# Moving one head's gate projection behind the last retention projection, and three tables behind the first weight loads

## The chip, the cores and the metric

The program runs on one core of one Trainium2 chip, in one launch. The metric is the device time of the program in microseconds (us); several executions are timed and the median is taken. TensorE multiplies matrices, VectorE and ScalarE work on whole tiles of 128 partitions, GpSimd takes a share of the elementwise work, and SyncE issues nearly all transfers between HBM and SBUF. Each engine runs its own instructions strictly in the order in which they stand in its program, and waits on semaphores for the others.

## What is computed

Two layers of a hybrid encoder over 512 tokens of width 1024. Each layer has four retention heads and four stick-breaking attention heads of width 128 that share one input projection and one output projection, then a SwiGLU feed-forward part; norms stand ahead of each part, and one more at the end.

```python
for l in range(DEPTH):                       # 2
    h = rms_norm(x, norm1_g[l])
    rq, rk, rv, rg, sq, sk, sv = jnp.split(h @ w_in[l], IN_SPLITS, axis=-1)   # 512 columns each
    ret = chunk_retention(apply_rotary(heads(rq)), apply_rotary(heads(rk)), heads(rv))
    ret = from_heads(head_group_norm(ret, ret_norm_g[l])) * jax.nn.silu(rg)
    sb  = stick_breaking(heads(sq), heads(sk), heads(sv))
    sb  = from_heads(head_rms_norm(sb, sb_norm_g[l]))
    x = x + jnp.concatenate([ret, sb], axis=-1) @ w_out[l]
    h = rms_norm(x, norm2_g[l])
    x = x + (jax.nn.silu(h @ w_gate[l]) * (h @ w_up[l])) @ w_down[l]
return rms_norm(x, final_g)
```

The gate `rg` has one block of 128 columns for each retention head. A head's gate is wanted only when that head's retention output is there, since `silu(rg)` multiplies it.

## The kernel before

Everything is float32. To reach that precision each operand is split into a high part (`hi`, a cast on ScalarE) and a low part (`lo`, a subtraction, on VectorE or GpSimd), and each product of two operands is three matmuls: hi·hi, lo·hi, hi·lo. The normed input stands in `hhi`, `hlo` (eight tiles of 128x512). The weights come in units of 512 KB, each of 128x1024, in the order of their use (`block_plan`). A unit is loaded into `wraw` (three buffers), cast to `whi` by ScalarE (L124) and subtracted to `wlo` by VectorE (L125). A cast must wait until TensorE has done with the unit that lay three units earlier in the same buffer.

In a layer's attention the order of TensorE's work is written out by hand. The main stream is: values of the stick-breaking heads (SV); for each stick head its query, key, and one retention gate (SQ, SK, RG); values of the retention heads (RV); for each retention head its query and key (RQ, RK); then the output projection, first the half of the stick heads, then that of the retention heads. One projection of a head is 24 matmuls of 512 columns and one unit of weights. Side tasks are put into this stream by the class `Stream`: a task is queued with a delay (`pe.later`) and written into TensorE's order when the stream has advanced so far. Heads are counted from 0 to 3.

The side tasks of retention head h are:

- `retain`: block `z` = scores of keys and queries, ten groups in three PSUM banks. The first matmul reads the high parts `qhi`, `khi`; the third is the first to read `klo`. VectorE then multiplies by the decay table `dec` (L552), and the product is split into `pthi`, `ptlo`.
- `mixed` (L557): `o` = values times weights, then VectorE's `m` = `o` times gain times gate (L561), and `normed`: ScalarE squares `o` (L460), casts the square to `shi`, GpSimd takes `slo`.
- `finish`: two matmuls of `ones_r` with `shi` and `slo` sum the squares into `o`; then `rsqrt`: on ScalarE a logarithm (L298) and an exponential (L299), both written as `r`, on VectorE `u`, `u`, `rn`; then `m` is scaled and split into `mhi`, `mlo` for the output projection.

Ahead of `retain`, `rotated` evacuates each query or key projection with three VectorE operations (L414 to L416, tiles `t`), GpSimd adds them, ScalarE casts (`qhi`, `khi`), GpSimd subtracts (`qlo`, `klo`).

ScalarE's functions come from table sets. A SiLU needs one set, logarithm and exponential another; `table_set` puts an explicit load into the program, and where a function stands under a set that doesn't hold it, another load is put in front of it. All four gates are passed through SiLU by one instruction of 2048 columns between two loads (L217, L220).

The order of TensorE is fixed by hand; that of VectorE, ScalarE, GpSimd and SyncE is set by a scheduler when the program is built. The two decay tables that fit (`dec`, two buffers) are loaded head by head in each layer (L537); the rotary tables `cosrs`, `sinrs` at the start of each layer's attention (L340, L341).

Of the kernel before, what the change touches and what calls it, by code (L numbers as in the profile page):

```python
# [10 lines left out]
F32 = mybir.dt.float32  # L11
# [3 lines left out]
ALU = mybir.AluOpType  # L15
# [9 lines left out]
NH = 4  # L25
# [11 lines left out]
# the triangle of score blocks, by bank: block rows of [query, key], and of [key, query]  # L37
# [7 lines left out]
def block_plan():  # L45
    """Weight blocks in the order of their use: (tensor, layer, k tile, column, width)."""
    plan = []

    def cols(name, l, col):
        return [(name, l, k, col, P) for k in range(KT)]  # L50

    for l in range(L):
        plan += [("w_in", l, k, SV, 512) for k in range(KT)]
        for h in range(NH):
            for c in (SQ, SK, RG):
                plan += cols("w_in", l, c + h * HD)
        plan += [("w_in", l, k, RV, 512) for k in range(KT)]
        for h in range(NH):
            plan += cols("w_in", l, RQ + h * HD) + cols("w_in", l, RK + h * HD)
        for d in range(KT):  # L60
            plan += [("w_out", l, NH + k, d * P, P) for k in range(NH)]
        for d0 in range(0, KT, 4):
            ds = range(d0, d0 + 4)
            plan += [("w_out", l, k, d * P, P) for d in ds for k in range(NH - 1)]
            plan += [("w_out", l, NH - 1, d * P, P) for d in ds]
        for k in range(KT):
            for f in range(2):
                plan += [("w_gate", l, k, f * P, P), ("w_up", l, k, f * P, P)]
        for half in range(2):
            fs = range(half * FH, half * FH + FH)  # L70
            for f in fs:
                if f >= 2:
                    plan += cols("w_gate", l, f * P) + cols("w_up", l, f * P)
            if l < L - 1:
                for d in range(KT):
                    plan += [("w_down", l, f, d * P, P) for f in fs]
            else:
                for dh in range(2):
                    plan += [("w_down", l, f, dh * 512, 512) for f in fs]
    return plan  # L80
# [13 lines left out]
class WeightStream:  # L94
    """Loads the weights ahead of their use and splits each into two 12-bit parts."""
# [10 lines left out]
    def load(self, upto, step=UW):  # L106
        for i in range(len(self.raw), min(upto, len(self.units))):
            w = sum(b[4] for b in self.units[i])
            raw = self.pool.tile([P, UW], F32, tag="wraw", name=f"wraw{i}", bufs=3)
            for a in range(0, w, step):  # L110
                c = slice(a, min(a + step, w))
                self.nc.sync.dma_start(out=raw[:, c], in_=self.ws[i, :, c])
            self.raw.append((raw, w))
# [28 lines left out]
class Stream:  # L142
    """The order of the tensor engine's work: side tasks are put into the main stream
    when enough of it has passed for their operands to be ready."""
# [54 lines left out]
def layers(ctx, tc, xT_in, ws_in, gcol_in, gfin_in, cos_in, sin_in, dec_in, out):  # L199
# [11 lines left out]
    def table(inst):  # L211
        """Keeps the scalar engine's table functions in the order of the program."""
        tc.stamp_issue_order_token(inst.ins, "table")
        return inst
# [42 lines left out]
    hlo = [keep.tile([P, S], F32R, name=f"hlo{k}", tag=f"hlo{k}") for k in range(KT)]  # L257
    ssq = keep.tile([P, S], F32, name="ssq")
# [23 lines left out]
    def feed(k, g):  # L282
        """x tile k is complete: its gained and split copy, and its squares."""
# [8 lines left out]
    def rsqrt(out, ss, n, act=nc.scalar.activation):  # L292
        """out = (ss / n + eps) ** -0.5, from exp and ln and a Newton step."""
# [16 lines left out]
    def token_scale():  # L310
        """rs[:, t] = rsqrt(mean of x[t]^2 + eps), the same on every partition."""
# [17 lines left out]
    def attention(l):  # L329
        g0 = l * NG  # L330
        with tc.tile_pool(name=f"at{l}", bufs=1, reuse_waits="tile") as sb:
# [7 lines left out]
            def scales():  # L339
                nc.sync.dma_start(out=cosrs, in_=cos_in)  # L340
                nc.sync.dma_start(out=sinrs, in_=sin_in)  # L341
# [15 lines left out]
            def proj_v(col, evac):  # L357
                """[token, column] products, the last k tiles by token block."""
# [62 lines left out]
            def outer(ps, a, b, ca, cb, last=True):  # L421
                """ps = a[:, ca].T @ b[:, cb] for split a and b."""
# [17 lines left out]
            def weighted(wt, v, h):  # L440
                """o[e, t] = sum over s of v[s, e] wt[s, t], by blocks of s."""
# [15 lines left out]
            def normed(o, m, key):  # L457
                """m, o by head with its gains, times the rsqrt of o's mean squares."""
# [76 lines left out]
            def retain(h, q, k, v):  # L535
                dec = sb.tile([P, S], F32, tag="dec", name="dec", bufs=2)
                nc.sync.dma_start(out=dec, in_=dec_in[:, h, :])  # L537
# [9 lines left out]
                for (z, n), js in zip(zs, BY_KEY):  # L547
                    pt, a = piece("p", F32, "pt", n, 3), 0
                    for j in js:
# [3 lines left out]
                            out=pt[:, c], in0=z[:, c], in1=dec[:, : S - j * P], op=ALU.mult  # L553
# [14 lines left out]

            gate = sb.tile([P, NH, S], F32, name="gate")
            v = proj_v(SV, evac_sv)  # L570
            for h in range(NH):
# [11 lines left out]
                ps = proj(RG + h * HD)  # L583
                nc.vector.tensor_tensor(out=gate[:, h], in0=ps, in1=rs, op=ALU.mult)

            def silu_gate():
                table_set(SILU)
                act(out=gate, in_=gate, func=AF.Silu)
                table_set(EXP_LN)

            v = proj_v(RV, evac_rv)
            pe.later(10000, silu_gate)
            for h in range(NH):
                q = rotated(proj(RQ + h * HD), "q")
                k = rotated(proj(RK + h * HD), "k")
                pe.later(D_RQK, lambda h=h, q=q, k=k, v=v: retain(h, q, k, v))

# [199 lines left out]
```

## Time and profile before

| What | Value |
|---|---|
| Time, median of 3 runs | 1240.82 us (1240.68 to 1240.99) |
| The profiled execution, its span | 1238.8 us |
| What lies around the span (median less span) | 2.0 us |
| TensorE busy | 1220.4 us, 99% of the span, 5474 matmuls |
| VectorE busy | 693.5 us, 56% |
| ScalarE busy | 488.8 us, 39% |
| GpSimd busy | 165.7 us, 13% |
| Mean granted TensorE clock | 0.994 of full speed |

The profiled execution has no time of its own beside its span; the 2.0 us are taken to lie around it in every execution. TensorE's busy time is modelled from pipelined matmuls, so that 99% only says that its gaps are few. Shares of the whole span hide that the stages differ: VectorE at 56% of the span is nearly full in some stretches. The second layer's attention repeats the first's, 607.63 us later.

### The profile page before, as it was taken

Reading aid. Unit: us, or ns where it says so; the run is one execution under the profiler, and the core shown is the slowest. Engines: PE = TensorE matmul, PEld = TensorE weight load, DVE = VectorE, ACT = ScalarE, POOL = GpSimd, SP = SyncE. Lnnn points to the kernel's source line nnn. Section 1 sums busy time; section 2 is a strip of 40 time slices with the busy share of each in tenths; the row PEclk is TensorE's granted clock in tenths of the full one; section 3 lists DMA queues with packets and bytes.
Section 4 is the critical chain, followed back from the end, with each engine's and each line's share of the span. In section 5 each row is a group of like instructions: output and inputs, shape, how many; then the busy total and the mean of one; then the engine's idle time right before and its main releaser. Section 6 shows DMA issues by size and latency. Waiting matters only on the chain.

```text
span 1238.8 us, 13898 instructions
## 1 busy us (share of the span) xinstructions
PE 1220.4 (99%) x5474; PEld 999.2 (81%) x5474; DVE 693.5 (56%) x861; ACT 488.8 (39%) x708; POOL 165.7 (13%) x142
## 2 busy tenths in 40 slices
PE   8999999999999999999999999999999999999997
PEld 5888887888888888888888888878888888888886
DVE  5557799775443244444444778997644433444433
ACT  5557553453322123223334766345432312223323
POOL 3221154130000000000112212422100000000011
PEclk9999999999999999999999999999999999999999
DMA  6221231232322323322232222223322322332221
GB/s 238 86 80 57 85 102 58 80 101 87 102 100 87 102 86 101 102 93 96 91 129 86 69 69 85 85 69 102 103 85 89 99 83 94 113 102 87 101 85 69
DMA packets 33329, 115.74 MB, mean 93 GB/s; under 512 B 3824, under 2 KB 3824, under 8 KB 33264
## 3 DMA queue, kind: packets, MB, share of 16 engines
q1 hardware_dynamic: 33120, 114.83, 28.1%
q8 instruction: 43, 0.70, 0.2%
q14 instruction: 22, 0.18, 0.0%
q10 hardware_dynamic: 144, 0.02, 0.0%
HBM read 112.75 MB, written 2.10 MB: 93 GB/s over the span
## 4 chain that ended last, share of the span: by engine, by line
PE 94%; DVE 4%; issue 1%; DMA 1%; ACT 1%; POOL 0%; SPq 0%; DVEq 0%; ACTq 0%
PE acc L178 72%; PE z L178 16%; PE o L178 5%; PE z L189 1%; DMA wraw<-ws 1%; DVE ptlo L274 1%; DVE wlo L125 1%; DVE hlo L277 0%; DVE u L300 0%; DVE mlo L274 0%; POOL slo L274 0%; DVE m L561 0%; DVE t L416 0%; DVE t L414 0%; DVE p L552 0%
## 5 line engine op out<-in xcount | busy, mean ns | idle before, releaser
L124 ACT CAST whi<-wraw 128x1024 fp32r<-128x1024 f32 (+1 forms) x205 | 214.6, 1047 | 505.7 <-PE acc L178 237.2
L178 PE MATMUL acc<-hhi,whi 128*128 128x512 f32 x960 | 376.0, 392 | 0.0
L178 PE MATMUL acc<-hhi,wlo 128*128 128x512 f32 x960 | 373.9, 389 | 0.0
L178 PE MATMUL acc<-hlo,whi 128*128 128x512 f32 x960 | 373.6, 389 | 0.0
L125 DVE TENSOR_TENSOR wlo<-wraw,whi 128x1024 fp32r<-128x1024 f32 (+1 forms) x205 | 258.1, 1259 | 135.8 <-ACT whi L124 134.7
L178 PEld LDWEIGHTS acc<-hhi,wlo 128*128 128x128 f32 x960 | 180.2, 188 | 37.8
L178 PEld LDWEIGHTS acc<-hhi,whi 128*128 128x128 f32 x960 | 180.3, 188 | 36.2
L178 PEld LDWEIGHTS acc<-hlo,whi 128*128 128x128 f32 x960 | 180.3, 188 | 36.0
L665 DVE TENSOR_TENSOR u<-acc,rs 128x512 f32<-128x512 f32 x40 | 27.7, 692 | 134.5 <-PE acc L178 134.5
L290 POOL TENSOR_TENSOR ssq<-ssq,sqx 128x512 f32<-128x512 f32 x28 | 44.8, 1600 | 397.0 <-ACT sqx L289 396.3
L662 DVE TENSOR_TENSOR g<-acc,rs 128x512 f32<-128x512 f32 x40 | 27.7, 692 | 89.9 <-PE acc L178 89.9
L178 PE MATMUL acc<-ahi,wlo 128*128 128x512 f32 x176 | 69.8, 396 | 0.0
L178 PE MATMUL acc<-alo,whi 128*128 128x512 f32 x176 | 69.8, 396 | 0.0
L178 PE MATMUL acc<-ahi,whi 128*128 128x512 f32 x176 | 69.8, 396 | 0.0
L730 POOL TENSOR_TENSOR xtd<-xtd,gfin 128x512 f32<-128x512 f32 x7 | 10.1, 1447 | 349.3 <-ACT fsq L726 349.3
L277 DVE SCALAR_TENSOR_TENSOR hlo<-x,gcol,hhi 128x512 fp32r<-128x512 f32 x32 | 38.6, 1224 | 9.0 <-ACT hhi L276 9.0
L178 PEld LDWEIGHTS acc<-alo,whi 128*128 128x128 f32 x176 | 33.1, 188 | 8.1
L178 PEld LDWEIGHTS acc<-ahi,whi 128*128 128x128 f32 x176 | 33.1, 188 | 8.1
L178 PEld LDWEIGHTS acc<-ahi,wlo 128*128 128x128 f32 x176 | 33.1, 188 | 8.1
L273 ACT CAST ahi<-u 128x512 fp32r<-128x512 f32 x44 | 27.3, 621 | 28.1 <-DVE u L666 28.1
L178 PE MATMUL acc<-mhi,wlo 128*128 128x512 f32 x88 | 36.2, 411 | 0.0
L178 PE MATMUL acc<-mlo,whi 128*128 128x512 f32 x88 | 36.0, 409 | 0.0
(189 smaller groups left out, 1819.0 us busy)
## 6 DMA issues: line engine op xcount, KB each, us to landing
wraw<-ws SPq DMA_DIRECT2D x203, 512.0 KB, 3.5
x<-xT SPq DMA_DIRECT2D x8, 256.0 KB, 7.4
dec<-dec SPq DMA_DIRECT2D x8, 256.0 KB, 4.1
out<-ob SPq DMA_DIRECT2D x4, 512.0 KB, 2.6
wraw<-ws SPq DMA_DIRECT2D x2, 256.0 KB, 3.8
cosrs<-cos SPq DMA_DIRECT2D x2, 256.0 KB, 5.3
sinrs<-sin SPq DMA_DIRECT2D x2, 256.0 KB, 5.4
gfin<-gfin SPq DMA_DIRECT2D x1, 512.0 KB, 4.5
```

Of the source, the lines that this page charges most:

```text
L124: nc.scalar.copy(out=hi[:, c], in_=raw[:, c])
L125: nc.vector.tensor_tensor(out=lo[:, c], in0=raw[:, c], in1=hi[:, c].bitcast(F32), op=ALU.subtract)
L178: self.nc.tensor.matmul(ps, lhsT=lhsT, rhs=rhs, start=start, stop=stop)
L189: self.nc.tensor.transpose(out, src, ident)
L273: nc.scalar.copy(out=hi, in_=src)
L274: eng.tensor_tensor(out=lo, in0=src, in1=hi.bitcast(F32), op=ALU.subtract)
L277: eng.scalar_tensor_tensor(out=lo, in0=src, scalar=scale, in1=hi.bitcast(F32), op0=ALU.mult, op1=ALU.subtract,)
L290: nc.gpsimd.tensor_tensor(out=ssq, in0=ssq, in1=q, op=ALU.add)
L662: nc.vector.tensor_tensor(out=g, in0=pg, in1=rs, op=ALU.mult)
L665: nc.vector.tensor_tensor(out=u, in0=pu, in1=rs, op=ALU.mult)
L730: nc.gpsimd.tensor_tensor(out=y, in0=y, in1=gfin[:, c], op=ALU.mult)
```

## The change

The gate projection of the last retention head leaves the stick-breaking part and stands behind the last key projection RK of the retention heads (`proj_gate(NH - 1)`). Its weights move to the same place in `block_plan`. The SiLU of the gates becomes two: one of 1536 columns for heads 0 to 2 at the old delay, and one of 512 columns for head 3 that is issued right behind its projection, each between two `table_set` calls. The four decay tables are loaded by one transfer of 1 MB in the first layer and kept; `cosrs`, `sinrs` and this transfer are issued behind the last weight load that is out at that time. A parameter of the program's constructor sets a scratch size.

```diff
     for l in range(L):
         plan += [("w_in", l, k, SV, 512) for k in range(KT)]
         for h in range(NH):
-            for c in (SQ, SK, RG):
+            for c in (SQ, SK, RG) if h < NH - 1 else (SQ, SK):
                 plan += cols("w_in", l, c + h * HD)
         plan += [("w_in", l, k, RV, 512) for k in range(KT)]
         for h in range(NH):
             plan += cols("w_in", l, RQ + h * HD) + cols("w_in", l, RK + h * HD)
+        plan += cols("w_in", l, RG + (NH - 1) * HD)
...
-                self.nc.sync.dma_start(out=raw[:, c], in_=self.ws[i, :, c])
+                self.last = self.nc.sync.dma_start(out=raw[:, c], in_=self.ws[i, :, c])
...
+    dec = keep.tile([P, NH, S], F32, name="dec")
...
             def scales():
-                nc.sync.dma_start(out=cosrs, in_=cos_in)
-                nc.sync.dma_start(out=sinrs, in_=sin_in)
+                with tc.issue_after(wst.last.ins):
+                    nc.sync.dma_start(out=cosrs, in_=cos_in)
+                    nc.sync.dma_start(out=sinrs, in_=sin_in)
+                    if l == 0:
+                        nc.sync.dma_start(out=dec, in_=dec_in)
...
             def retain(h, q, k, v):
-                dec = sb.tile([P, S], F32, tag="dec", name="dec", bufs=2)
-                nc.sync.dma_start(out=dec, in_=dec_in[:, h, :])
...
-                            out=pt[:, c], in0=z[:, c], in1=dec[:, : S - j * P], op=ALU.mult
+                            out=pt[:, c], in0=z[:, c], in1=dec[:, h, : S - j * P], op=ALU.mult
...
+            def proj_gate(h):
+                ps = proj(RG + h * HD)
+                nc.vector.tensor_tensor(out=gate[:, h], in0=ps, in1=rs, op=ALU.mult)
...
-                ps = proj(RG + h * HD)
-                nc.vector.tensor_tensor(out=gate[:, h], in0=ps, in1=rs, op=ALU.mult)
-
-            def silu_gate():
+                if h < NH - 1:
+                    proj_gate(h)
+
+            def silu_gate(hs):
                 table_set(SILU)
-                act(out=gate, in_=gate, func=AF.Silu)
+                act(out=gate[:, hs], in_=gate[:, hs], func=AF.Silu)
                 table_set(EXP_LN)
 
             v = proj_v(RV, evac_rv)
-            pe.later(10000, silu_gate)
+            pe.later(10000, lambda: silu_gate(slice(0, NH - 1)))
             for h in range(NH):
                 q = rotated(proj(RQ + h * HD), "q")
                 k = rotated(proj(RK + h * HD), "k")
                 pe.later(D_RQK, lambda h=h, q=q, k=k, v=v: retain(h, q, k, v))
+            proj_gate(NH - 1)
+            silu_gate(slice(NH - 1, NH))
...
-    nc = bacc.Bacc("TRN2", target_bir_lowering=False, num_devices=1)
+    nc = bacc.Bacc("TRN2", target_bir_lowering=False, num_devices=1, dynamic_dma_scratch_size=1024)
```

The scheduler makes new orders of this. Three places are shown, each before and after, first layer; the numbers behind names are those of buffers, and the second layer has the same order.

ScalarE, around the SiLU of the gates, before: `whi25` are the weights of RK of head 2, `khi_1451` the high part of head 0's key, which `retain` of head 0 reads.

```order
L220 ACT_TABLE_LOAD
L217 ACTIVATE gate_205<-gate_205 128x2048
L220 ACT_TABLE_LOAD
L124 CAST whi24_1456<-wraw24_1415 128x1024
L273 CAST mhi_1383<-m_1313 128x512
L273 CAST qhi_1406<-q_1404 128x512
L124 CAST whi25_1498<-wraw25_1460 128x1024
L273 CAST khi_1451<-k_1449 128x512
```

After (weights of one projection fewer have passed, so that RK of head 2 is `whi24`):

```order
L275 CAST qhi_1360<-q_1358 128x512
L301 ACTIVATE r_1387<-r_1387 128x512
L125 CAST whi23_1426<-wraw23_1369 128x1024
L125 CAST whi24_1468<-wraw24_1430 128x1024
L275 CAST mhi_1395<-m_1330 128x512
L221 ACT_TABLE_LOAD
L218 ACTIVATE gate_206<-gate_206 128x1536
L221 ACT_TABLE_LOAD
L275 CAST khi_1421<-k_1419 128x512
```

The load, the SiLU and the load have moved from ahead of three casts to between the weights of RK of head 2 and head 0's `khi`.

ScalarE behind the last key projection, before: the two `r` are the logarithm and the exponential of head 1's `finish`, `khi_1879` is head 3's key.

```order
L124 CAST whi30_1884<-wraw30_1775 128x1024
L298 ACTIVATE r_1860<-o_1856,eps_111 128x512
L299 ACTIVATE r_1860<-r_1860 128x512
L124 CAST whi31_1918<-wraw31_1888 128x1024
L273 CAST mhi_1868<-m_1796 128x512
L273 CAST khi_1879<-k_1877 128x512
```

After (the same `r`, `mhi` and `khi` under new numbers; `gate` of 512 columns is head 3's):

```order
L125 CAST whi29_1848<-wraw29_1741 128x1024
L221 ACT_TABLE_LOAD
L300 ACT_TABLE_LOAD
L300 ACTIVATE r_1824<-o_1820,eps_111 128x512
L301 ACT_TABLE_LOAD
L301 ACTIVATE r_1824<-r_1824 128x512
L125 CAST whi30_1883<-wraw30_1852 128x1024
L218 ACT_TABLE_LOAD
L218 ACTIVATE gate_206<-gate_206 128x512
L221 ACT_TABLE_LOAD
L275 CAST mhi_1832<-m_1762 128x512
L275 CAST khi_1843<-k_1841 128x512
```

Five table loads and the SiLU have come in: the explicit load of the SiLU's set stands ahead of head 1's logarithm, so that logarithm, exponential and SiLU each get a load of their own.

TensorE at the end of the last key projection, before: `o_1856` takes the sum of squares of head 1, `mhi`, `mlo` are stick heads in the output projection.

```order
L178 MATMUL acc_1770<-hlo7_133,whi27_1616 128x512
L178 MATMUL acc_1770<-hhi7_125,wlo27_1617 128x512
L178 MATMUL o_1856<-shi_1800,ones_r_109 128x512
L178 MATMUL o_1856<-slo_1801,ones_r_109 128x512
L178 MATMUL acc_1883<-mhi_796,whi28_1713 128x512
L178 MATMUL acc_1883<-mlo_797,whi28_1713 128x512
```

After:

```order
L179 MATMUL acc_1736<-hlo7_133,whi26_1584 128x512
L179 MATMUL acc_1736<-hhi7_125,wlo26_1585 128x512
L179 MATMUL o_1820<-shi_1766,ones_r_109 128x512
L179 MATMUL o_1820<-slo_1767,ones_r_109 128x512
L179 MATMUL acc_1847<-hhi0_118,whi27_1679 128x512
L179 MATMUL acc_1847<-hlo0_126,whi27_1679 128x512
```

The 24 matmuls of the moved gate projection (`acc_1847`) stand behind the two sums of head 1, ahead of the first output products. Behind them TensorE has the same number of matmuls as before up to the score block `z` of head 3. VectorE evacuates the gate behind head 3's three `t` operations and ahead of head 1's scaling of `m`. On SyncE, weight units 4 to 6 now stand ahead of `cosrs`, `sinrs` and `dec`, and unit 7 behind them.

## Rows read from the trace of the kernel before

**Rows 1.** windows of 20 us: busy us and instructions of each engine, clock, DMA

```profile
20.00:40.00 20.00, 16.96 (x71) 13.76 (x72) 12.76 (x18) 7.62 (x12) 3.94 (x3) 0.91 0.30 97
...
200.00:220.00 20.00, 17.66 (x76) 14.02 (x75) 19.28 (x27) 10.19 (x17) 7.76 (x5) 0.91 0.18 67
...
800.00:820.00 20.00, 17.38 (x73) 13.95 (x74) 19.08 (x25) 7.40 (x12) 6.59 (x5) 0.91 0.19 67
```

**Rows 2.** TensorE in order of time: start, us, instruction, [idle before, releaser]

```profile
23.77 0.79 PE L178 MATMUL z<-wlo,hhi 128*128 128x512 f32 x1 [2.74 <-DVE wlo L125]
...
192.66 0.50 PE L178 MATMUL o<-pthi,vhi 128*128 128x512 f32 x1 [0.42 <-DVE u L303]
...
202.05 0.49 PE L178 MATMUL o<-shi,ones_r 128*128 128x512 f32 x1 [1.29 <-ACT shi L273]
203.60 0.50 PE L178 MATMUL o<-slo,ones_r 128*128 128x512 f32 x1 [1.05 <-POOL slo L274]
```

**Rows 3.** the chain that ended last: start, us, what, TensorE pieces

```profile
36.16 16.32 PE acc L178 x72
...
204.10 7.84 PE acc L178 x27
...
229.92 4.20 PE acc L178 x18
```

**Rows 4.** the table loads of the program: nanoseconds min/median/max, first and last start

```profile
L220 ACT ACT_TABLE_LOAD  x9: 1283/1283/1283, 1.2 to 1171.9; - x9
```

**Rows 5.** ScalarE in order of time, around the SiLU of the gates

```profile
154.12 1.28 ACT L220 ACT_TABLE_LOAD   x1
155.42 1.92 ACT L217 ACTIVATE gate<-gate 128x2048 f32<-128x2048 f32 x1
...
162.91 1.05 ACT L124 CAST whi<-wraw 128x1024 fp32r<-128x1024 f32 x1 [2.17 <-PE acc L178]
164.38 0.62 ACT L273 CAST khi<-k 128x512 fp32r<-128x512 f32 x1 [0.42 <-POOL k L418]
```

**Rows 6.** GpSimd in order of time: the low parts of the first and last keys

```profile
165.08 1.30 POOL L274 TENSOR_TENSOR klo<-k,khi 128x512 fp32r<-128x512 f32 x1 [0.73 <-ACT khi L273]
...
214.38 1.50 POOL L274 TENSOR_TENSOR klo<-k,khi 128x512 fp32r<-128x512 f32 x1 [0.73 <-ACT khi L273]
```

**Rows 7.** TensorE: third products of the first and of the last score block

```profile
167.48 0.39 PE L178 MATMUL z<-qhi,klo 128*128 128x512 f32 x1
...
216.24 0.39 PE L178 MATMUL z<-qhi,klo 128*128 128x512 f32 x1
```

**Rows 8.** ScalarE in order of time, after the last key projection

```profile
203.25 1.04 ACT L124 CAST whi<-wraw 128x1024 fp32r<-128x1024 f32 x1
204.20 0.68 ACT L298 ACTIVATE r<-o,eps 128x512 f32<-128x512 f32 x1
204.91 0.63 ACT L299 ACTIVATE r<-r 128x512 f32<-128x512 f32 x1
211.04 1.05 ACT L124 CAST whi<-wraw 128x1024 fp32r<-128x1024 f32 x1 [5.50 <-PE acc L178]
```

**Rows 9.** VectorE in order of time, first layer, retention

```profile
180.54 0.75 DVE L561 SCALAR_TENSOR_TENSOR m<-o,gcol,gate 128x512 f32<-128x512 f32 x1 [1.29 <-PE o L178]
...
206.58 0.68 DVE L300 SCALAR_TENSOR_TENSOR u<-r 128x512 f32<-128x512 f32 x1
...
209.08 0.69 DVE L306 SCALAR_TENSOR_TENSOR rn<-u,r 128x512 f32<-128x512 f32 x1
...
211.09 0.68 DVE L416 TENSOR_TENSOR t<-acc,sinrs 64x512 f32<-64x512 f32 x1
```

**Rows 10.** work that covers the moved loads and the token scale, GpSimd and VectorE

```profile
33.43 1.30 POOL L347 TENSOR_TENSOR cosrs<-cosrs,rs 128x512 f32<-128x512 f32 x1 [12.06 <-DVE rst L306]
...
31.21 0.77 DVE L300 SCALAR_TENSOR_TENSOR u<-r 128x512 f32<-128x512 f32 x2 [5.75 <-ACT r L217]
```

**Rows 11.** DMA issues, page: KB each, median us from issue to landing

```profile
cosrs<-cos SPq DMA_DIRECT2D x2, 256.0 KB, 5.3
```

## The prediction

> **What bounds the kernel now.** I read the windows first. TensorE, in the first column, is busy for nearly all of every slice; it loses time in three places only, and those are the slices where the granted clock is 0.91 as well [rows 1]: the start, and the same stretch of each layer's retention part (200 to 220 us and 800 to 820 us). There VectorE, third column, is full (19.28 and 19.08 of 20). So everywhere else the time is TensorE's matmul count, and an edit gains or loses only where it makes or closes a hole on TensorE.
>
> TensorE in order of time gives the holes [rows 2]. At the start 2.74 us pass before a low part of weights comes from VectorE. In the first layer's retention part TensorE waits 0.42 us for VectorE's `u`, then, at the end of the last key projection, 1.29 us for `shi` and 1.05 us for `slo` of head 1. VectorE is what is late there: head 1's `m` (L561) comes late, and the squaring waits behind it. After that wait 27 matmuls take 7.84 us, while 18 of the same kind take 4.20 later [rows 3]: 27 x 0.2333 = 6.30, so 1.54 us went to the low clock. One layer's retention holes cost 0.42 + 1.29 + 1.05 + 1.54 = 4.3 us, both layers 8.6 us (0.7%).
>
> Working time: the span is 1238.8 us and 2.0 us lie around it; I add the changes of the span to the median, 1240.8. In what follows clock times are those of the trace of before. Behind the move the same matmuls stand some 5.5 us earlier (24 of them have moved past), which doesn't change a difference.
>
> **Edits that I cost at nothing.** TensorE runs the same matmuls, so the moved projection costs 24 matmuls less ahead of RV and 24 more behind RK of head 3: zero. Its eviction on VectorE is one operation like `t`, 0.68 us [rows 9], and is counted below, where it matters.
>
> The loads: the last of the three weight units now ahead of `cosrs` can go out when the low part has been made that TensorE waits for at 23.77 [rows 2], so `cosrs` and `sinrs` go out near 24. With the 5.3 us of landing [rows 11] they are there near 30; GpSimd multiplies them by `rs` at 33.43, after 12.06 us of waiting for VectorE [rows 10]. The cover is about 3 us; without it GpSimd, then the first rotated query, come later by the excess, with all stick heads in between, so still 0. Weight unit 7 queues behind 1 MB of `dec`: four times 256 KB, at worst 4 x 5.3 = 21 us after 25. Unit 7 holds the fourth projection, which begins when three projections of 24 matmuls (16.32 us from 36.16 [rows 3]) are done, at 52.5. At the start one weight subtraction also comes ahead of the token scale's low part; VectorE idles 5.75 us right after that [rows 10], so a shift of some 1.2 us is covered. The eight `dec` loads that go were off TensorE's path. The start's hole stays: the operations ahead of it are the same. No row depends on the scratch size; every load in the rows is issued by SyncE. All this: 0.
>
> **Term 1: the first score block.** The SiLU with its two loads now stands between the cast of RK of head 2's weights and head 0's `khi`. Today the cast starts at 162.91, when TensorE releases the buffer, and `khi` comes at 164.38, right after it and GpSimd's sum [rows 5]; `klo` takes 1.30 on GpSimd [rows 6], and TensorE's third matmul of `z`, the first that reads `klo`, starts at 167.48 [rows 7]. The release is by the same matmul after the change (the end of RQ of head 1), so the new chain hangs on it: cast 1.05, `mhi` 0.62 (as `khi`, the same form), load 1.28 [rows 4], SiLU of 1536 columns 1.92 x 3/4 = 1.44 [rows 5], load 1.28, `khi` 0.62, `klo` 1.30: 7.59, and about 0.2 for seven hand-overs (load at 154.12 to SiLU at 155.42 is 1.30 for 1.283). The third matmul starts at 162.91 + 7.8 = 170.7 instead of 167.48: TensorE loses **3.2 us**, most of it ahead of the block, the rest behind its second matmul. Bounds: 3.0 without the hand-overs; 3.7 if `klo` is slowed to some 1.8 by VectorE, as an estimate from 1.50 against 1.30 [rows 6]. Queued behind the SiLU on ScalarE is just `khi`; who waits is TensorE, then VectorE for the products.
>
> **Term 2: the last score block.** Behind the last key projection the cast `whi` ends at 203.25 + 1.04 = 204.3, and head 1's logarithm and exponential start at 204.20 and 204.91 [rows 8]. After, two loads come first: 204.3 + 2.57 = 206.9; logarithm 0.68, load 1.28, exponential 0.63: done at 209.5. VectorE's `u` follows, at 209.55 instead of 206.58 [rows 9]. Now `u`, `u`, `rn` (0.7 each, as `rn` at 209.08 is 0.69 long) to 211.6, three `t` of 0.7 to 213.7 (today the last starts at 211.09), the gate's eviction to 214.3. SiLU of 512 columns 0.62 (as `khi`; the loads that come ahead of it are done at 211.04 + 1.05 + 1.28 = 213.4, since the cast at 211.04 waits for the same count of matmuls) to 214.95, load to 216.2, `mhi` and `khi` to 217.45, `klo` 1.50 to 219.0. TensorE's third matmul of head 3's `z` starts at 216.24 today [rows 7]: it loses **2.8 us**. Bounds: 2.4 if `klo` takes 1.30 and the hand-overs nothing; 3.5 if GpSimd and VectorE slow each other. Later needs (products of head 3, last sums) have the moved 24 matmuls as cover and add nothing.
>
> **The old holes** stay. VectorE waits 1.29 us for TensorE ahead of head 0's `m` at 180.54 [rows 9]; whatever lead it has is lost there, and from there to the hole at the end of RK of head 3 both engines have the same work as before. The moved gate stands behind that hole, not in it.
>
> **The clock.** All three waits of over 2 us in total were followed by a clock of half speed, costing some 1.5 us each [rows 1, 2, 3]. The four new waits (two per layer) are as long, but broken up by two matmuls. Four falls would add 6.2; if the new pauses shift the old ones so that their falls go, -3.1. I take one fall net, +1.5: nearer to the new waits' rows than to none, but not four, since they are broken up.
>
> **Sum:** 2 x (3.2 + 2.8) + 1.5 = 13.5; 1240.8 + 13.5 = **1254.3**, rounded 1254.
>
> **A rule of the Trainium skill.** The SiLU starts 1.30 us after the start of the load ahead of it [rows 5]. The Trainium skill (ScalarE: Activation LUTs, section "What ACT_TABLE_LOAD costs") gives 1283 ns for the load and about 1380 ns of drain on top, 2.66 us for each switch. The row has the load's 1.28 and no drain. By the rule term 1 would grow by 2 x 1.38 and term 2 by 5 x 1.38, in all 2 x 9.7 = 19.3 more.
>
> **Rivals.** (a) The moved matmuls fill the holes of retention: the 8.6 us go, 1232.2. For it: the gate's eviction leaves a crowded VectorE. Against it: the order puts the gate behind the sums, and VectorE resynchronises at 180.54. It decides if head 1's `slo` comes 2.3 us earlier against TensorE. This is the one on the faster side. 0.04. (b) Both new waits come, but TensorE, held at the first block, lets VectorE run ahead and the old holes close: 1240.8 + 12.0 - 8.6 = 1244.2. Against it the same 1.29 us. 0.06. (c) Only one of the two waits comes, because the other chain is hidden by something that I take as late: 1240.8 + 2 x 3.2 = 1247.2 or 1246.4. 0.07. (d) The loads are hidden altogether, ScalarE being idle for 5.50 us ahead of 211.04 [rows 8]: 1240.8. It would need the casts behind the loads to be early; they are just in time. 0.05. (e) Each switch costs a drain too: 1273.6. 0.02.
>
> **How the numbers follow.** My forecast has 0.76, with its own range 1249 (bounds low, falls lost) to 1260 (bounds high, four falls). The range of 8 in 10 reaches from it to (c): 1246 to 1260. A measurement can tell 0.2%, 2.5 us. Faster is (a), 0.04; same is (d) and part of (b), 0.06; slower is the rest, 0.90.
>
> **What would show it.** In the profile after: nine table loads become nineteen; TensorE has waits on ScalarE's `khi` and GpSimd's `klo` at the first and at the last score block of each layer, together near 3 us each; the waits on `shi` and `slo` at the end of RK of head 3 are as today. If head 0's `khi` doesn't wait for the second load, or if the exponential's lateness doesn't reach `khi` of head 3, a term is wrong. If TensorE waits there under 1 us, the forecast is.

## The result and the profile after

The changed kernel takes **1259.0 us** (median of 4 runs, 1258.06 to 1262.9) beside 1240.75 us for the kernel before: a ratio of 1.0157, 95% interval 1.0141 to 1.0173. It is slower, as forecast. The median lies inside the stated 1246 to 1260, near its upper end; the ratio times 1240.82 gives 1260.3, which is past that end by 0.3. The forecast was 1254.3, so 4.7 us of the slowdown were not foreseen.

The page of the kernel after: the span, the first line of busy times (microseconds, share of the span, instructions), and from the groups of instructions the four with table loads (count | busy us, mean ns | idle before).

```profile
span 1257.0 us, 13895 instructions
PE 1229.0 (98%) x5474; PEld 1004.4 (80%) x5474; DVE 691.0 (55%) x861; ACT 503.0 (40%) x720; POOL 165.6 (13%) x142
...
L221 ACT ACT_TABLE_LOAD x13 | 16.7, 1283 | 1.4 <-PEq L796 1.2
...
L300 ACT ACT_TABLE_LOAD x2 | 2.6, 1283 | 0.0
L301 ACT ACT_TABLE_LOAD x2 | 2.6, 1283 | 0.0
L218 ACT ACT_TABLE_LOAD x2 | 2.6, 1283 | 0.0
```

The nine loads of [rows 4] have become 13 + 2 + 2 + 2 = 19, each as long as before. TensorE runs the same 5474 matmuls.

TensorE's waits of the kernel after, by the engine waited for (us in total, times, longest us):

```profile
PE z L179 <- ACT khi L275: 8.8, 4, 2.6
PE o L179 <- ACT shi L275: 2.6, 2, 1.3
...
PE o L179 <- POOL slo L276: 2.1, 2, 1.1
...
PE z L179 <- POOL klo L276: 1.2, 3, 0.6
```

The first and the last line are new: four waits for `khi` and behind them three for `klo`, at the first and the last score block of each layer. The waits for `shi` and `slo` are those of [rows 2], unchanged.

TensorE of the kernel after in order of time, first layer and then two rows of the second; the columns are those of [rows 2] and [rows 7]:

```profile
162.82 0.50 PE L179 MATMUL z<-qhi,khi 128*128 128x512 f32 x1 [2.64 <-ACT khi L275]
...
164.18 0.50 PE L179 MATMUL z<-qhi,klo 128*128 128x512 f32 x1 [0.62 <-POOL klo L276]
...
200.52 0.50 PE L179 MATMUL o<-shi,ones_r 128*128 128x512 f32 x1 [1.31 <-ACT shi L275]
202.07 0.51 PE L179 MATMUL o<-slo,ones_r 128*128 128x512 f32 x1 [1.05 <-POOL slo L276]
...
216.13 0.59 PE L179 MATMUL z<-qhi,khi 128*128 128x512 f32 x1 [1.76 <-ACT khi L275]
...
217.48 0.80 PE L179 MATMUL z<-qhi,klo 128*128 128x512 f32 x1 [0.33 <-POOL klo L276]
...
781.42 0.80 PE L179 MATMUL z<-qhi,klo 128*128 128x512 f32 x1
...
835.39 0.80 PE L179 MATMUL z<-qhi,klo 128*128 128x512 f32 x1 [0.26 <-POOL klo L276]
```

From the chain that ended last, the first 72 projection matmuls of each layer after, and under them those of the second layer before:

```profile
34.53 16.32 PE acc L179 x72
...
651.75 16.32 PE acc L179 x72
```

```profile
643.74 16.32 PE acc L178 x72
```

With these the 18.2 us of span (1257.0 - 1238.8) can be laid out. Until the end of each layer's output projection the kernel after has done 24 matmuls fewer at the same place (a third of the 72 above, 16.32 / 3 = 5.44 us), so 5.44 is added to the three differences inside retention; the first and the last row need nothing added.

| Event, layer 0 | before | after | difference, with the 5.44 | new since the event above |
|---|---|---|---|---|
| first 72 projection matmuls | 36.16 [rows 3] | 34.53 | -1.63 | -1.63 |
| third product of the first score block | 167.48 [rows 7] | 164.18 | 2.14 | **3.77**, wait |
| sum of head 1 reads `shi` | 202.05 [rows 2] | 200.52 | 3.91 | **1.77**, clock |
| third product of the last score block | 216.24 [rows 7] | 217.48 | 6.68 | **2.77**, wait |
| first 72 projection matmuls of layer 1 | 643.74 | 651.75 | 8.01 | **1.33**, clock |

In the second layer the same steps are 3.76, 2.41, 2.77 and 1.25 (the rows of before there are at 775.09, 809.68 and 823.88). Together: start -1.63, waits 13.07, the stretches behind the waits 6.76; 18.2. The 13.07 us are how late the third product is. They are more than the 10.0 us of waits listed above (8.8 + 1.2), since TensorE fills a part of the lateness with the two products ahead of it. The second kind of time is the clock: in the windows of 20 us of the kernel after (busy us of PE, PEld, DVE, ACT, POOL; then the granted clock, DMA share, GB/s; [rows 1] are those of before),

```profile
20.00:40.00 20.00, 18.07 (x84) 14.75 (x83) 12.52 (x17) 7.94 (x13) 3.69 (x3) 1.00 0.51 188
...
160.00:180.00 20.00, 16.73 (x73) 13.79 (x73) 14.25 (x19) 7.83 (x11) 7.46 (x5) 0.91 0.22 69
...
200.00:220.00 20.00, 16.35 (x62) 12.71 (x63) 15.73 (x19) 15.06 (x19) 7.41 (x5) 0.83 0.15 53
```

the clock is below full speed in 160 to 180, where the kernel before has 1.00, and 0.83 instead of 0.91 in 200 to 220: a second fall there, at the last score block. At the start, the other way, it stays full where [rows 1] has 0.91. That is most of the 1.63: the wait at the start ends at 23.53 instead of 23.77, 0.24 us earlier, and the other 1.4 us come behind it.

### The profile page after: what moved, and what is told of

Its sections match the earlier page's. It is cut to its first block, busy times and chain, and to the rows that moved or that the text cites. A ratio compares the mean times of both kernels' runs of the same rounds, so it can differ in the third digit from the quotient of the medians.

```text
span 1257.0 us, 13895 instructions
## 1 busy us (share of the span) xinstructions
PE 1229.0 (98%) x5474; PEld 1004.4 (80%) x5474; DVE 691.0 (55%) x861; ACT 503.0 (40%) x720; POOL 165.6 (13%) x142
## 4 chain that ended last, share of the span: by engine, by line
PE 90%; DVE 4%; issue 2%; POOL 2%; ACT 1%; DMA 1%; SPq 0%; DVEq 0%; POOLq 0%; ACTq 0%
PE acc L179 69%; PE z L179 16%; PE o L179 4%; PE z L190 1%; DVE wlo L126 1%; DVE ptlo L276 1%; DMA wraw<-ws 1%; DVE u L302 1%; POOL k L423 0%; POOL slo L276 0%; POOL klo L276 0%; DVE hlo L279 0%; POOL q L423 0%; DVE t L420 0%; DVE t L421 0%
## 5 line engine op out<-in xcount | busy, mean ns | idle before, releaser
L126 DVE TENSOR_TENSOR wlo<-wraw,whi 128x1024 fp32r<-128x1024 f32 (+1 forms) x205 | 255.0, 1245 | 142.4 <-ACT whi L125 141.2
L276 POOL TENSOR_TENSOR slo<-sq,shi 128x512 fp32r<-128x512 f32 x16 | 23.8, 1489 | 89.9 <-ACT shi L275 89.8
L278 ACT ACTIVATE hhi<-x,gcol 128x512 fp32r<-128x512 f32 x32 | 22.8, 718 | 30.7 <-DVE x L714 14.6
```

Of the source, the lines that this page charges most:

```text
L126: nc.vector.tensor_tensor(out=lo[:, c], in0=raw[:, c], in1=hi[:, c].bitcast(F32), op=ALU.subtract)
L276: eng.tensor_tensor(out=lo, in0=src, in1=hi.bitcast(F32), op=ALU.subtract)
L278: nc.scalar.activation(out=hi, in_=src, func=AF.Copy, scale=scale)
```

## The experiments

Theory: the slowdown is the place of the two SiLUs with their table loads in ScalarE's order, ahead of a `khi` that TensorE wants, with a fall of the clock behind each wait; the moved projection and the moved loads are neutral. Rivals: the loads carry part of it; the moved projection does; each table switch costs wherever it stands; the falls of the clock have nothing to do with the waits. All times below stand beside 1240.2 to 1240.6 us for the kernel before on the same chip.

**The moved loads alone.** To the kernel before, `dec` loaded once and kept, it and `cosrs`, `sinrs` behind the weight loads, and the scratch size (the main lines of the edit):

```diff
+                with tc.issue_after(wst.last.ins):
+                    nc.sync.dma_start(out=cosrs, in_=cos_in)
+                    nc.sync.dma_start(out=sinrs, in_=sin_in)
+                    if l == 0:
+                        nc.sync.dma_start(out=dec, in_=dec_in)
```

> The kernel before with the moved loads alone: decay tables loaded once, they and cosrs, sinrs behind the last weight load; all four gates projected and passed through SiLU as before. Theory (the slowdown is ScalarE's table loads ahead of khi; the loads moved cost nothing): 1240.8 us, or 1239.2 if the smaller first hole of the changed kernel (1.9 us instead of 2.74, and no fall of the clock behind it) comes from the loads. Retention as before: waits on shi and slo, 2.4 us, in each layer, none on khi. Rival (the moved loads cost a part of the 18 us, through weight unit 7 behind 1 MB): over 1243.

Measured: 1240.56 us, ratio 0.9998 (0.9989 to 1.0006). The loads cost and give nothing that shows: the interval is about 1 us to either side. The windows of this kernel, columns as above:

```profile
20.00:40.00 20.00, 16.96 (x65) 13.59 (x66) 12.00 (x18) 6.69 (x11) 3.93 (x3) 0.83 0.41 154
200.00:220.00 20.00, 17.13 (x79) 13.49 (x79) 19.77 (x27) 9.33 (x16) 7.60 (x6) 1.00 0.24 80
800.00:820.00 20.00, 17.19 (x80) 13.63 (x80) 19.54 (x26) 8.45 (x13) 6.48 (x5) 1.00 0.23 78
```

They show two things. The hole at the start is 2.75 us again and the clock stays low behind it for some 6.8 us, where the kernel before has 3.4 (0.83 and 0.91 in the window), so the 1.63 us gained there by the profiled execution of the changed kernel are not the loads'. And the waits for `shi` and `slo` are there in both layers (2.7 and 2.1 us in all), but no fall follows them (1.00 in both rows), where the kernel before had one in each layer [rows 1].

**The moved projection without the moved loads.** The changed kernel with `dec`, `cosrs`, `sinrs` loaded and the scratch size set as before (the main lines of the edit):

```diff
-                with tc.issue_after(wst.last.ins):
-                    nc.sync.dma_start(out=cosrs, in_=cos_in)
...
+                dec = sb.tile([P, S], F32, tag="dec", name="dec", bufs=2)
+                nc.sync.dma_start(out=dec, in_=dec_in[:, h, :])
```

> The changed kernel without the moved loads: gate projection and second SiLU moved, the decay tables loaded head by head as before. Theory: all of the slowdown stays, and the start is again as in the kernel before: per layer 3.77 + 2.82 us of lateness at the first and last score block and two falls of the clock at some 1.7 us, in all 2 x 10 = 20, so 1260.7 us. Rival (the loads carry some of it): under 1256.

Measured: 1259.91 us, ratio 1.0159 (1.0146 to 1.0173). All of the slowdown is here, and its waits are the changed kernel's (8.9 us for `khi` in four, 1.2 for `klo`). The first hole is 2.74 us again.

**The first SiLU one cast earlier.** The changed kernel with one number changed:

```diff
-            pe.later(10000, lambda: silu_gate(slice(0, NH - 1)))
+            pe.later(14000, lambda: silu_gate(slice(0, NH - 1)))
```

> The changed kernel with the SiLU of heads 0 to 2 queued at a delay of 14000 instead of 10000, which puts it one weight cast earlier on ScalarE, into the 4.17 us in which ScalarE waits ahead of the cast of RK of head 2; nothing else of the arithmetic differs. Theory: load 1.28, SiLU 1.49, load 1.28 fit into the 4.17 us, khi of head 0 comes in time, the wait of 3.77 us a layer goes and the fall of the clock behind it (5.5 and 5.8 us by layer): 1259.0 - 11.3 = 1247.7 us. Rival 1 (the falls of the clock have another cause than the waits): 1259.0 - 7.5 = 1251.5. Rival 2 (something else than the SiLU holds head 0's khi, or VectorE's lateness behind it takes the gain): 1256 to 1259, with longer waits on shi and slo of head 1.

Measured: 1247.76 us, ratio 1.006 (1.0047 to 1.0074); 11.2 us less than the changed kernel. ScalarE in order of time, first in the changed kernel, then in this one:

```profile
155.91 1.06 ACT L125 CAST whi<-wraw 128x1024 fp32r<-128x1024 f32 x1 [4.17 <-PE acc L179]
157.42 0.62 ACT L275 CAST mhi<-m 128x512 fp32r<-128x512 f32 x1 [0.45 <-DVE m L476]
158.06 1.28 ACT L221 ACT_TABLE_LOAD   x1
159.36 1.49 ACT L218 ACTIVATE gate<-gate 128x1536 f32<-128x1536 f32 x1
160.86 1.28 ACT L221 ACT_TABLE_LOAD   x1
162.15 0.62 ACT L275 CAST khi<-k 128x512 fp32r<-128x512 f32 x1
```

```profile
151.77 1.28 ACT L221 ACT_TABLE_LOAD   x1
153.06 1.49 ACT L218 ACTIVATE gate<-gate 128x1536 f32<-128x1536 f32 x1
154.57 1.28 ACT L221 ACT_TABLE_LOAD   x1
155.95 1.05 ACT L125 CAST whi<-wraw 128x1024 fp32r<-128x1024 f32 x1
...
158.59 0.62 ACT L275 CAST khi<-k 128x512 fp32r<-128x512 f32 x1 [0.54 <-POOL k L423]
```

The same three instructions now fill the 4.17 us in which ScalarE waited for TensorE to release a weight buffer. The cast behind them comes 0.04 us later and `khi` 3.56 us earlier. The wait at the first block is gone in both layers; the one at the last block is still there. The lateness at the first block was 7.5 us in both layers, so 3.7 us of the gain are more than that: the falls of the clock went with it (none follows the first block in this profile), and the rival that has them independent of the waits (1251.5) did not come.

**The second SiLU behind head 3's `khi`.** The changed kernel with

```diff
-            silu_gate(slice(NH - 1, NH))
+            pe.later(4200, lambda: silu_gate(slice(NH - 1, NH)))
```

> The changed kernel with the SiLU of head 3 queued 4200 later, which puts it and its two loads behind head 3's khi and score products on ScalarE, and takes away the three loads that logarithm and exponential of head 1 forced. Theory: the wait at the last score block (2.82 us a layer) goes with its fall of the clock, 4.15 and 4.4 us by layer: 1259.0 - 8.5 = 1250.5 us; the wait at the first block stays. Rival 1 (falls independent of the waits): 1259.0 - 5.6 = 1253.4. Rival 2 (the SiLU, now close to its use, delays head 2's logarithm or head 3's m, and a new wait behind it takes back most): 1256 or more.

Measured: 1249.98 us, ratio 1.0079 (1.0066 to 1.0092); 9.0 us less than the changed kernel. The third product of the last score block runs without a wait in layer 0, and the SiLU stands where ScalarE has done head 3's `pthi`:

```profile
217.20 0.39 PE L179 MATMUL z<-qhi,klo 128*128 128x512 f32 x1
```

```profile
221.42 0.63 ACT L218 ACTIVATE gate<-gate 128x512 f32<-128x512 f32 x1
```

No wait of TensorE over 0.21 us has come in for it; the wait at the first block is still there.

**Both.** The two edits together:

> The changed kernel with both moves of the two runs before it: the SiLU of heads 0 to 2 one cast earlier, that of head 3 behind head 3's khi. Gate projection, second SiLU and moved loads stay. Theory (the place of the SiLUs on ScalarE is the whole slowdown, and the moved 24 matmuls are neutral): the two gains add, 11.2 and 9.0, so 1259.0 - 20.2 = 1238.8, near 1240 us, with the waits on shi and slo of head 1 as in the kernel before. Rival (the moved projection has a cost of its own, by VectorE's extra eviction or by the second SiLU so late): over 1243.

Measured: 1241.26 us, ratio 1.0007 (0.9998 to 1.0016). With the moved projection, the second SiLU and four more table loads all still in, the slowdown is gone. TensorE's waits of this kernel hold no `khi` and no `klo`:

```profile
PE o L179 <- ACT shi L275: 2.6, 2, 1.3
PE o L179 <- POOL slo L276: 2.1, 2, 1.1
```

The sum of the two single gains had promised 1238.8. In the profiled executions of the two single edits the waits for `shi` and `slo` were followed by a fall of the clock in one layer of two; here, as in the kernel before, in both. Each of the single gains may then hold a fall that its edit had no part in, and two falls are more than the 2.5 us missing; but it is one execution of each, so this is not shown.

**Only the split.** The kernel before, its SiLU in two parts, the second queued behind the last key projection:

```diff
+            pe.later(10000, lambda: silu_gate(slice(0, NH - 1)))
...
+            silu_gate(slice(NH - 1, NH))
```

> The kernel before with its SiLU split in two and nothing else: gates of all heads projected as before, SiLU of heads 0 to 2 as before, SiLU of head 3 queued behind the last key projection. The order then has it behind head 3's khi, with two loads more a layer. Theory (a switch costs by its place): 1240.8 us. Rival (each switch costs its loads or more wherever it stands): four loads of 1.28 more, 1246 or above.

Measured: 1243.83 us, ratio 1.0029 (1.0019 to 1.0039). Neither expectation was met: not free, and under four loads. Again it is what the order puts behind the SiLU. Here the SiLU and its second load stand ahead of head 2's square, and two casts of `pthi` have come in between the square and `shi`; ScalarE and, below, TensorE in order of time:

```profile
215.34 0.63 ACT L217 ACTIVATE gate<-gate 128x512 f32<-128x512 f32 x1
...
217.29 0.60 ACT L460 ACTIVATE sq<-o 128x512 f32<-128x512 f32 x1
218.05 1.28 ACT L273 CAST pthi<-p 128x512 fp32r<-128x512 f32 x2 [0.17 <-DVE p L552]
219.24 0.61 ACT L273 CAST shi<-sq 128x512 fp32r<-128x512 f32 x1
```

```profile
219.91 0.50 PE L178 MATMUL o<-shi,ones_r 128*128 128x512 f32 x1 [0.35 <-ACT shi L273]
221.39 0.50 PE L178 MATMUL o<-slo,ones_r 128*128 128x512 f32 x1 [0.98 <-POOL slo L274]
```

In the kernel before `shi` follows the square at once (217.12 and 217.76, where everything is 0.27 us later than here). Here the square is 0.4 us late and `shi` 1.75 us, so the sum of head 2 waits 1.33 us in this layer and 0.54 + 0.99 in the other: 2.9 us of the 3.6 measured.

**The chain to the last block, cut in half.** The changed kernel with logarithm and exponential of the heads' norms kept in program order among the table functions:

```diff
-                    rsqrt(rn, ss, HD)
+                    rsqrt(rn, ss, HD, act)
```

> The changed kernel with logarithm and exponential of the heads' norms kept in the order of the program among ScalarE's table functions. Behind the last key projection they then stand ahead of the second SiLU's load, and three of the five loads there go; the first SiLU stays where it is. Theory (the lateness at the last score block is a chain through those loads, VectorE's u and the gate's eviction to khi): the chain is shorter by 1.8 of its 2.82 us, since cast, load and khi still stand behind a SiLU that waits for the gate: 1259.0 - 3.6 = 1255.4, or down to 1252 if falls of the clock go with it. Rival (the three loads lie in time that ScalarE has anyway, and only the SiLU and the load behind it count): 1258 to 1260, the wait at the last block unchanged.

Measured: 1251.52 us, ratio 1.0087 (1.0075 to 1.01); 7.5 us less than the changed kernel, half a microsecond beyond the far end of what the theory allowed. In the changed kernel ScalarE runs, behind the last key projection and the cast of weights there:

```profile
202.78 1.28 ACT L221 ACT_TABLE_LOAD   x1
204.07 1.28 ACT L300 ACT_TABLE_LOAD   x1
205.36 0.69 ACT L300 ACTIVATE r<-o,eps 128x512 f32<-128x512 f32 x1
206.07 1.28 ACT L301 ACT_TABLE_LOAD   x1
207.36 0.63 ACT L301 ACTIVATE r<-r 128x512 f32<-128x512 f32 x1
```

With the edit, cast, logarithm and exponential follow each other and one load stands behind them. TensorE at the last score block of layer 0 then waits

```profile
214.28 0.50 PE L179 MATMUL z<-qhi,khi 128*128 128x512 f32 x1 [0.51 <-ACT khi L275]
215.64 0.50 PE L179 MATMUL z<-qhi,klo 128*128 128x512 f32 x1 [0.62 <-POOL klo L276]
```

1.13 us, where the changed kernel waits 1.76 + 0.33 = 2.09; and no fall of the clock follows. So the exponential's lateness does reach `khi` of head 3, through VectorE's queue. In layer 1 TensorE doesn't wait for `khi` there at all: its clock had fallen just ahead of it, behind the wait for `slo` (0.83 in 815 to 825), and a slower TensorE meets `khi` in time.

**The old hole, first attempt.** The kernel before with the moved loads and head 1's two sums queued later, behind output products:

```diff
-                pe.later(D_SS, finish)
+                pe.later(D_SS + wait, finish)
...
-                    normed(o, m, h)
+                    normed(o, m, h, 3000 if h == 1 else 0)
```

> The kernel before with the moved loads and with the two sums of head 1's squares queued 3000 later, which puts them behind a dozen products of the output projection on TensorE. Theory (TensorE waits 1.3 and 1.05 us for shi and slo there because the sums come too early, VectorE being late): the wait goes in both layers, 2 x 2.35 = 4.7, and up to 3.4 with the falls of the clock that follow it: 1240.6 - 4.7 = 1235.9, down to 1232.5. Rival (the later sums make head 1's logarithm and u late, and the product of head 2's weights and values waits for the bank that they hold): 1239 or more.

Measured: 1249.17 us, ratio 1.007 (1.0057 to 1.0082): the rival, and more of it than it had. The waits for `shi` and `slo` are gone, but in ScalarE's new order head 1's logarithm stands behind head 3's `khi`, which waits 5.67 us for its operand; VectorE's second `u` frees the bank of the sums late, and TensorE waits for it ahead of head 2's weighted sum:

```profile
209.91 0.62 ACT L274 CAST khi<-k 128x512 fp32r<-128x512 f32 x1 [5.67 <-POOL k L422]
210.44 0.68 ACT L299 ACTIVATE r<-o,eps 128x512 f32<-128x512 f32 x1
```

```profile
213.76 0.80 PE L178 MATMUL o<-pthi,vhi 128*128 128x512 f32 x1 [5.24 <-DVE u L304]
```

The same edit on the kernel with both SiLUs moved:

> The changed kernel with both SiLUs moved and with head 1's sums 3000 later. Theory: as the kernel before with the later sums, 1232.5 to 1236, since the moved projection is neutral once its SiLU is out of the way. Rival 1 (the moved projection fills VectorE's crowded stretch less, so that still more holes close): under 1232. Rival 2 (gate of head 3 and its SiLU come too late for head 3's m when TensorE is faster): over 1238.

Measured: 1250.11 us, ratio 1.0078 (1.0065 to 1.0091). The theory failed here for the same reason (6.42 us of waiting for the second `u`), not by either rival.

**The old hole, second attempt.** The kernel before with the moved loads, and one low part less on VectorE:

```diff
-                    split(hi, lo, m)
+                    split(hi, lo, m, eng=nc.gpsimd if key in (0,) else nc.vector)
```

> The kernel before with the moved loads, and with head 0's mlo taken by GpSimd instead of VectorE (1.77 us, right ahead of head 1's m; GpSimd is idle for 3.7 us at that time). Theory (the hole at the end of the last key projection is VectorE's lateness with head 1's m, and nothing of the change touched that): m, square, shi and slo of head 1 come 1.8 to 2.3 us earlier, so of the 2.35 us of waiting under 0.6 are left; 1240.6 less 3.6 to 4.6, less up to 3.4 for falls of the clock: 1233 to 1237. Rival (GpSimd's own work behind it, q of head 2 and slo, is late by the same amount, or VectorE slows): 1239 or more.

Measured: 1236.44 us, ratio 0.9971 (0.9959 to 0.9983): 0.3% faster than the kernel before. Head 0's `mlo` stands on GpSimd at 195.48 for 1.29 us, VectorE reaches head 1's `m` at 197.92 instead of 199.49, and of the two waits 0.30 us is left:

```profile
201.43 0.50 PE L178 MATMUL o<-slo,ones_r 128*128 128x512 f32 x1 [0.30 <-POOL slo L275]
...
213.77 0.50 PE L178 MATMUL z<-qhi,klo 128*128 128x512 f32 x1 [0.82 <-POOL klo L275]
```

The second row is what is late next: TensorE, now ahead, meets head 3's `klo` 0.82 us early. By the waits the gain is 2 x 2.05 less 2 x 0.82, 2.5 us, of 4.1 measured; no fall of the clock follows these shorter waits, which can account for the rest, as an estimate from one execution.

The same edit on the changed kernel with both SiLUs moved:

> The changed kernel with both SiLUs moved (as in e5_both) and head 0's mlo on GpSimd. Theory: as e9_mlo_pool within 1 us, since the moved projection is neutral; 1233 to 1237. Rival (the moved projection gives the faster stretch something that the kernel before doesn't have, or takes it): over 2 us from e9_mlo_pool either way.

Measured: 1236.52 us, ratio 0.997 (0.9959 to 0.9982). The same 0.33 and 0.79 us are left, and the two medians are within 0.1 us, their intervals about 1.5 us to either side: where the gate of head 3 is projected makes no difference that these runs can tell.

## Why the prediction was right, and where it was wrong

**What bounds the kernel**, and that an edit counts only where it opens a hole on TensorE: right. With both SiLUs in other places all the rest of the change is worth 0.0007 of the time.

**Edits costed at nothing**: right. The moved loads gave 0.9998 by themselves, and the moved projection nothing (1236.44 and 1236.52). The gain at the start was not foreseen. It goes with the fall of the clock that is missing there: the kernel with the first SiLU earlier has the hole at its full 2.75 us, no fall behind it, and starts the 72 projections at 34.55, as the changed kernel does at 34.53.

**Term 1** was sized too low: 3.2 us forecast, 3.77 and 3.76 measured, just over the upper bound of 3.7. The chain ran as written, cast, `mhi`, load, SiLU, load, `khi`, `klo`, at 155.91 to 164.18, 8.27 us where 7.8 were counted. The link left out is in the row of `mhi`: 0.45 us of waiting for VectorE's `m`.

**Term 2**: 2.8 us forecast, 2.77 measured in both layers. VectorE's first `u` stands at 208.03, against 209.55 less the 1.5 us by which VectorE is earlier there (head 1's `m` at 197.96 instead of 199.49). Behind it two small errors cancel, which is luck: the SiLU starts 0.2 us later than counted, and `klo` takes 1.27 us instead of 1.50. That the exponential's lateness reaches `khi`, which the prediction named as the weak link, was tried by itself: without the three loads the waits at the last block of layer 0 go from 2.09 to 1.13 us.

**The old holes** stay: right, 1.31 and 1.05 us as before. They are VectorE's, as argued, since one operation less on VectorE takes 2.05 of the 2.35 us away. Giving TensorE other work ahead of the sums closed them too, but opened waits of 5.24 us for VectorE's `u` instead.

**The clock** is the step that failed. The prediction took one net fall, +1.5 us, because the new waits are "broken up by two matmuls". Four new ones came, worth 1.77, 1.33, 2.41 and 1.25: **6.76 us**, and one old one, at the start, was missing in this execution, most of the 1.63 us given back. The price of a fall was about right (1.69 in the mean), the count was not, and being broken up was no reason: in the profiled executions of the five kernels that have new waits of 2 us and more (2.0 to 3.3 us, in one or two pieces), a fall follows 14 of 14. The prediction had both ends in hand (four falls, 6.2) and took the wrong one. What decides whether a fall comes stays open.

**The sum**: 13.1 + 6.8 - 1.6 = 18.2 measured, 12.0 + 1.5 = 13.5 forecast; of the difference 1.1 is term 1 (0.9 of it the wait for `m`), 3.6 the clock and the start. The stated upper end doesn't follow from its parts: bounds high and four falls give 1240.8 + 2 x (3.7 + 3.5) + 6.2 = 1261.4, not 1260. And the middle terms with four falls would have given 1240.8 + 12.0 + 6.2 = 1259.0, the measured median, but in part by luck, since term 1's excess and the gain at the start work against each other.

**The rivals.** (a) and (b), closed holes, didn't come: the waits for `shi` and `slo` are as before. (c), one wait only, is what the kernels with one SiLU moved are; their 1247.8 and 1250.0 are 1.4 and 2.8 us above the prediction's 1246.4 and 1247.2, which count no falls. (d), loads hidden altogether at 1240.8, is what both edits together give, 1241.26: the time was there on ScalarE, one cast earlier and one step later. (e) didn't come: in the changed kernel loads that follow each other start 1.29 us apart (202.78, 204.07) and the logarithm 1.29 us after the second, and `khi` 1.29 after the load at 160.86. The Trainium skill (ScalarE: Activation LUTs, section "What ACT_TABLE_LOAD costs") has about 1380 ns of drain on top of the 1283 ns of a load, which by an estimate from that figure would be 2 x 1.38 = 2.8 us in the chain to the first `khi`. The rows do not bear the drain out.

## What to carry to other kernels

Work added to an engine that is 40% busy can cost more than its own length when it is put into the order just ahead of something that the bounding engine wants: here ScalarE's busy time grew by 14.2 us (503.0 less 488.8) and the span by 18.2. Look for the idle stretch a few instructions earlier or later, and move the work there by whatever number sets its place. Price a new wait on TensorE with the fall of the clock that may follow it: here 13.1 us of lateness came to 19.8 us. And a hole that a full engine makes is better closed by taking work off that engine; giving the waiting one something else first moved the wait here and made it longer.

## What the runs showed of the hardware

**A fall of TensorE's clock behind a wait is not certain.** The same pair of waits for `shi` and `slo` (1.3 + 1.05 us) is in nine of the profiled kernels, in both layers: of the 18 pairs 12 were followed by a stretch at 1.2 GHz (granted clock 0.50 in windows of 2 us) and 6 stayed at 2.4. The single hole at the start, 2.75 us, was followed by no fall in two of the kernels (the first SiLU earlier, and both SiLUs moved with the sums later), and by one in the kernel before. The waits of the change, 2.0 to 3.3 us in all, were followed by one 14 times of 14, so it is not their total length alone that decides; what does was not tried. The profiled executions of the kernel before and of the one with the moved loads alone have nearly the same span (1238.8 and 1239.2 us), though the first had both falls in retention and the second neither, with 1.5 us more at the start: one execution's count of falls is not the kernel's.

**A fall also hides.** Where the clock fell just ahead of the last score block (layer 1 of the kernel whose logarithm and exponential come first), TensorE no longer waited for `khi` there, and where it didn't fall, as with the moved loads alone, a wait of 0.49 us for `klo` appeared that the kernel before doesn't have. So gains of single edits that touch such waits don't add exactly: 11.2 and 9.0 us alone, 17.7 together.

**Logarithm and exponential** each got a table load of their own when they stood behind the SiLU's set (L300, L301 in the rows above), though in [rows 8] they run without any load between them. With the load that the SiLU then needed (L218) that is three loads a layer that no line of the program asks for.
